# The values of a gated linear attention turned in 32x32 squares and through device memory, in place of TensorE transposes

## The chip, the cores and the metric

The kernel runs on one core of one Trainium2 chip. A core has TensorE (PE in the profile: matmuls; PEld: loads of its weights), VectorE (DVE), ScalarE (ACT), GpSimd (POOL) and SyncE (SP), which here issues nearly all transfers. Engines work side by side, each through its own list of instructions. The metric is the time of one execution in microseconds (us); lower is better.

## The reference, cut to what matters

Two layers of an encoder over 272 rows (256 tokens and 16 meta tokens), width 2048, in fp32. Each layer projects the stream once, runs gated linear attention (4 heads, key width 128, value width 256) beside a neighbourhood attention (16 heads), projects back, and ends with a squared-ReLU MLP of width 8192.

```python
proj = jnp.einsum('bld,dp->blp', h, w_in)
gq, gk, gv, gr, glr, nq, nk, nv = jnp.split(proj, points, axis=-1)
...
scores = jnp.einsum('bhtd,bhsd,bhtsd->bhts', qi, ki, decay)
intra = jnp.einsum('bhts,bhse->bhte', scores, vi)
```

The change concerns `gv`, the values: 4 heads of 256 columns. The projection makes them with the columns on the 128 partitions and the 272 rows along a partition; the product with the scores wants them the other way round, rows on the partitions.

## The kernel before

**Weights.** All weights come in tiles of 128 x 1024 floats (512 KB), always in the same way. SP loads a tile into `raw` (`made`, L195). ACT rounds it to the fast matmul type as `wh` (L218), DVE makes the remainder `wl` (L219). `raw`, `wh` and `wl` have three buffers each, so SP can load a tile only when DVE is done with the tile three before it, and ACT can convert a tile only when PE is done with the tile three before it. `weights` keeps two tiles ready ahead of the one in use.

**Projection.** `by_m` makes 128 columns at a time: two weight tiles, each used by `eight` (L253) for 8 blocks with three matmuls per block (`wh` on the high part of the stream, `wh` on its low part, `wl` on the high part), 24 matmuls in all. In the second layer, where only 256 rows are wanted, the q columns take two matmuls per block, `wh` and `wl` in turn, 16 in all. The order inside a tile is "hlhlww" or "hwhw...": the first kind needs `wl` at the fifth matmul, the second at the second.

**The stage around the change.** For each layer, `by_k` makes the keys and the first four value chunks (c0 to c3), then `by_m` makes the value chunks c4 to c7 and after them the four q chunks. In what follows the weight tiles of these `by_m` runs are numbered: T0 and T1 make c4, T2 and T3 c5, T4 and T5 c6, T6 and T7 c7; T8 and T9 make the first q chunk, T10 and T11 the second. Between the tiles, `pump` lets other work take a step: the generator `gates` (the low-rank decays: a projection of 32 matmuls at L469, small matmuls at L487, and on ACT and DVE a chain of abs, exp, ln, min and exp per head, L488 to L493), and for each head `v_rows`.

**The values.** `ev_v` copies a chunk from PSUM to `ft` (L504). When both chunks of a head are there, `v_rows` transposes them on PE with an identity (6 matmuls a head, L517), and `split` and `stack` read the result from PSUM: ACT writes the high part `V` (L339), DVE the low part, which lies in the tiles y12 to y15 (L340); the 16 meta rows go to `VS`, twice high by ACT (L345) and once low by DVE (L346). `gla_head` uses them later as matmul weights (L716 to L720).

**Order.** Each engine's instructions stand in one list that the building framework makes from the code and from what each instruction depends on; waits are on counters that other engines and transfers raise. An engine works through its list from the front, so an instruction that waits holds up all that stand behind it. SP's list in this stage is hardly more than the loads of L195.

Of the kernel before, what the change touches and what calls it, by code (L numbers as in the profile page):

```python
# [38 lines left out]
PAD = 40  # L39
PITCH = 288  # L40
WIDE = 1280
HIGHS = {"once": (0, P, 2 * P), "two": (0, P, 2 * P), "all": (0, P, 2 * P), "all2": (0, P, 2 * P), "own2": (0, P + 48, 2 * P + 64)}
# [16 lines left out]
class Trunk:  # L59
# [127 lines left out]
    def made(self, ap, ends, kind):  # L187
        if ap is None:
            return None
        nc = self.nc  # L190
        raw = self.wp.tile([P, WB], F32, name="raw", tag="raw")
        wh, wl = (self.wp.tile([P, WIDE], F32R, name=nm, tag=nm) for nm in ("wh", "wl"))
        wh, wl = self.blocks(wh, *HIGHS[kind]), self.blocks(wl, *LOWS[kind])
        for c in map(slice, (0,) + ends, ends):
            nc.sync.dma_start(raw[:, c], ap[:, c])  # L195
# [157 lines left out]
    def layer(self, l):  # L353
# [4 lines left out]
        with ExitStack() as actx:  # L358
# [7 lines left out]
            self.decay = [t(f"dec{h}", [P, 2, L]) for h in range(GH)]  # L366
            self.V = a.tile([P, 2 * GH, 2, P], F32R, name="V", tag="V")
            self.vlow = [self.pair(self.yp, "y", 12 + h).both.rearrange("p a c -> p (a c)") for h in range(GH)]
            self.VS = a.tile([80, GH * GDV], F32R, name="VS", tag="VS")
            nc.gpsimd.memset(self.VS.bitcast(F32), 0.0)  # L370
            self.y, self.gate, self.done, self.vt = [None] * DC, {}, set(), []
            if l:
# [6 lines left out]
            with ExitStack() as ectx:  # L379
# [9 lines left out]
                for m, ps in enumerate(first):  # L389
                    self.ev_v(m, ps[0])  # L390
                self.credit, self.alone = 0, True
                self.by_m(self.x, [L] * 4, lambda m, ps: self.ev_v(4 + m, ps), pump=(1, 1, True))
                self.by_m(self.x, [n] * 4, self.ev_q, pump=(1, 1, True))
# [108 lines left out]
    def ev_v(self, c, ps):  # L502
        vt = self.ep.tile([P, L], F32, name="ft", tag="ft", bufs=4)
        self.nc.scalar.copy(vt, ps)  # L504
        self.vt.append(vt)
        if c % 2:
            (self.fg if c > 3 else self.bg).append(self.v_rows(c // 2, self.vt[-2:]))

    def v_rows(self, h, vt):

        nc = self.nc
        yield True
        pt = self.spare(2)
        for i in range(3):
            n = P if i < 2 else NM
            for e in range(2):
                nc.tensor.transpose(pt[e][:n, i * P:i * P + P], vt[e][:, i * P:i * P + n], self.ident)  # L517
# [61 lines left out]
    def gla_head(self, h):  # L579
# [132 lines left out]
        for e in range(2):  # L712
            o = self.bank()[:, :n]
            for i in range(2):
                v, vl = self.V[:, 2 * h + e, i, :], self.vlow[h][:, e * T + i * P:e * T + i * P + P]
                nc.tensor.matmul(o, lhsT=v, rhs=high[:, i, :], start=not i, stop=False)  # L716
# [469 lines left out]
def layout(inputs):  # L1186
# [95 lines left out]
```

## Time and profile before

| | |
|---|---|
| three executions | 2322.43, 2322.55, 2327.5 us; median 2322.55 us |
| profiled execution | 2326.07 us, its span 2324.3 us, mean granted TensorE clock 0.998 |
| PE busy | 2308.5 us (99%), weight loads 2192.0 us (94%) |
| DVE, ACT, POOL busy | 1536.8 us (66%), 1223.4 us (53%), 125.9 us (5%) |
| transfers | 431.65 MB, mean 186 GB/s |
| value and q stage, first layer | about 53 to 93 us |
| value and q stage, second layer | about 1242 to 1285 us |

A group's row in the profile names line, engine, operation, what is written and read, the shape and the count; behind the bar stand the busy time in us, the mean duration of one in ns, and the idle time of the engine just before them with what ended it. A row of the timeline has the start and the length in us, then the same names. In the rows of the windows the engines' busy time comes with the count of instructions in brackets, then the granted clock (PEclk).

### The profile page before, as it was taken

The numbers are of one execution on the slowest core, as the hardware profiler recorded it, in microseconds if no ns is written. First come the engines' busy times: TensorE is split into PE (matmuls) and PEld (weight loads), VectorE is DVE, ScalarE is ACT, GpSimd is POOL, SyncE is SP. The second block draws the span as 40 slices with busy tenths as digits, with TensorE's granted clock in tenths as the row PEclk, the third lists the DMA queues.
The fourth block names the chain that finished last, engine by engine and source line by source line (L and its number), as shares of the span: only waits on it lengthen the run. The fifth ranks groups of instructions, "written<-read, shape, count | busy, mean of one in ns | idle before, by whom it ended". The sixth has DMA issues, their size and how long they took to land.

```text
span 2324.3 us, 45263 instructions
## 1 busy us (share of the span) xinstructions
PE 2308.5 (99%) x18412; PEld 2192.0 (94%) x18412; DVE 1536.8 (66%) x2456; ACT 1223.4 (53%) x2096; POOL 125.9 (5%) x200
## 2 busy tenths in 40 slices
PE   9999999999999999999999999999999999999998
PEld 9999999999999999999999899989988888888888
DVE  5588887775544455557576788878866545666655
ACT  5666664564433344444456767655654334555443
POOL 0022100110000000000020011100100000000000
PEclk9999999999999999999999999999999999999999
DMA  8555665566665556666655656666666666666664
GB/s 258 155 164 184 196 187 169 170 185 179 179 180 181 182 178 178 180 181 179 179 179 164 181 173 204 210 185 182 198 192 193 192 195 191 192 197 218 195 196 148
DMA packets 129824, 431.65 MB, mean 186 GB/s; under 512 B 14792, under 2 KB 23496, under 8 KB 129616
## 3 DMA queue, kind: packets, MB, share of 16 engines
q1 hardware_dynamic: 117808, 415.65, 59.4%
q10 hardware_dynamic: 11808, 13.11, 1.7%
q8 instruction: 144, 2.36, 0.4%
q14 instruction: 64, 0.52, 0.1%
HBM read 420.32 MB, written 8.39 MB: 184 GB/s over the span
## 4 chain that ended last, share of the span: by engine, by line
PE 91%; DVE 5%; ACT 1%; issue 1%; DMA 1%; ACTq 0%; DVEq 0%; POOL 0%
PE mm L253 52%; PE mm L265 30%; PE mm L304 4%; PE mm L314 2%; DVE wl L219 2%; PE bg L304 1%; DMA raw<-in_win 1%; ACT wh L218 0%; PE bg L851 0%; DVE S L614 0%; PE bg L628 0%; PE bg L469 0%; DVE acc L423 0%; DVE ns L787 0%; ACT ns L756 0%
## 5 line engine op out<-in xcount | busy, mean ns | idle before, releaser
L219 DVE TENSOR_TENSOR wl<-raw,wh 128x1024 fp32r<-128x1024 f32 (+1 forms) x770 | 937.4, 1224 | 626.4 <-ACT wh L218 519.8
L218 ACT CAST wh<-raw 128x1024 fp32r<-128x1024 f32 (+1 forms) x770 | 805.3, 1047 | 757.7 <-PE mm L253 353.3
L253 PE MATMUL mm<-x,wh 128*128 128x272 f32 (+3 forms) x4544 | 806.1, 294 | 0.0
L253 PEld LDWEIGHTS mm<-x,wh 128*128 128x128 f32 x4544 | 647.1, 188 | 15.6 <-issue 0.5
L253 PE MATMUL mm<-x,wl 128*128 128x272 f32 (+3 forms) x2432 | 520.7, 284 | 4.0 <-DVE wl L219 3.9
L253 PEld LDWEIGHTS mm<-x,wl 128*128 128x128 f32 x2432 | 390.7, 188 | 5.5 <-DVE wl L219 5.5
L253 PE MATMUL mm<-y,wh 128*128 128x272 f32 (+1 forms) x1440 | 235.0, 285 | 0.0
L253 PEld LDWEIGHTS mm<-y,wh 128*128 128x128 f32 x1440 | 199.7, 188 | 0.1
L265 PE MATMUL mm<-x,wh 128*128 128x512 f32 x832 | 193.8, 390 | 0.0
L265 PEld LDWEIGHTS mm<-x,wh 128*128 128x128 f32 x832 | 154.3, 188 | 31.0
L253 PE MATMUL mm<-u,wh 128*128 128x272 f32 (+1 forms) x1056 | 172.1, 285 | 0.0
L265 PE MATMUL mm<-y,wh 128*128 128x512 f32 x688 | 162.3, 389 | 0.0
L265 PEld LDWEIGHTS mm<-y,wh 128*128 128x128 f32 x688 | 128.6, 188 | 26.9 <-issue 0.4
L253 PE MATMUL mm<-y,wl 128*128 128x272 f32 (+1 forms) x720 | 146.4, 284 | 0.0
L253 PEld LDWEIGHTS mm<-u,wh 128*128 128x128 f32 x1056 | 146.3, 188 | 0.0
L265 PE MATMUL mm<-u,wh 128*128 128x512 f32 x496 | 118.3, 391 | 0.0
L253 PEld LDWEIGHTS mm<-y,wl 128*128 128x128 f32 x720 | 112.5, 188 | 0.0
L265 PEld LDWEIGHTS mm<-u,wh 128*128 128x128 f32 x496 | 90.9, 188 | 17.7
L253 PE MATMUL mm<-u,wl 128*128 128x272 f32 (+1 forms) x528 | 107.3, 284 | 0.0
L265 PEld LDWEIGHTS mm<-x,wl 128*128 128x128 f32 x832 | 98.4, 188 | 2.0
L265 PE MATMUL mm<-x,wl 128*128 128x256 f32 x832 | 98.8, 276 | 0.0
L265 PEld LDWEIGHTS mm<-y,wl 128*128 128x128 f32 x688 | 84.3, 188 | 2.9
(273 smaller groups left out, 2274.9 us busy)
## 6 DMA issues: line engine op xcount, KB each, us to landing
raw<-in_wff SPq DMA_DIRECT2D x512, 512.0 KB, 3.6
raw<-in_win SPq DMA_DIRECT2D x190, 512.0 KB, 4.1
raw<-in_wout SPq DMA_DIRECT2D x64, 512.0 KB, 4.1
hop<-nt ACTq DMA_DIRECT2D x16, 384.0 KB, 2.4
np<-hop ACTq DMA_DIRECT2D x64, 96.0 KB, 4.8
nb<-in_nab SPq DMA_DIRECT2D x16, 352.0 KB, 4.9
xraw<-in_xT SPq DMA_DIRECT2D x7, 272.0 KB, 5.0
out<-out SPq DMA_DIRECT2D x5, 256.0 KB, 3.0
```

Of the source, the lines that this page charges most:

```text
L218: self.nc.scalar.copy(h, r)
L219: self.wl = self.nc.vector.tensor_tensor(lo, r, h.bitcast(F32), ALU.subtract).ins
L253: mm(o, lhsT=self.block(w, j), rhs=rhs, start=first and not i, stop=last and i == len(TURNS[once]) - 1)
L265: self.nc.tensor.matmul(o, lhsT=self.block(both[j // 8][low], j % 8), rhs=rhs, start=first and not i + j, stop=bool(last and i and j == 15 ...
L304: self.nc.tensor.matmul(ps[g + m][:, :n], lhsT=self.block(parts[p][0], 4 * j + m if first else 2 * m + j), rhs=acts[k + j][parts[p][1]][:, ...
L314: self.nc.tensor.matmul(o, lhsT=self.block(both[low], i), rhs=rhs, start=not low and k + i % 2 == 0, stop=k == DC - 2 and i % 2 == 1 and n ...
```

## The change

PE no longer transposes the values. `ev_v` copies a chunk into a buffer of 288 columns (GpSimd clears the last 16), and DVE turns it in 32x32 squares into `vt`. A new generator, `v_flow`, walks once through the heads with three kinds of steps: `w` writes a head's `vt` to device memory (one transfer on ACT's queue, 288 KB); `r` reads it back as rows, one transfer for each of the eight 32-row blocks (32 KB each, 256 bytes at a time) and one for the meta rows, all nine on SP's queue behind the last weight load asked for so far; `s` makes the high part on ACT, the low part in place on DVE, and `VS`. The steps are w0 w1 r0 w2 r1 s0 r2 w3 s1 r3 s2 s3. The meta rows `vm` have two buffers. The value columns of `w_in` are put in another order on the host, so that the squares come out right, and `gla_head` takes its slices from the new layout with the same matmuls.

```diff
@@ made
-            nc.sync.dma_start(raw[:, c], ap[:, c])
+            self.asked = nc.sync.dma_start(raw[:, c], ap[:, c]).ins
@@ layer
-            self.V = a.tile([P, 2 * GH, 2, P], F32R, name="V", tag="V")
+            self.V = a.tile([P, GH, 2, GDV], F32R, name="V", tag="V")
...
+                self.bg.append(self.v_flow())
                 self.by_m(self.x, [L] * 4, lambda m, ps: self.ev_v(4 + m, ps), pump=(1, 1, True))
@@ ev_v, v_rows
-        vt = self.ep.tile([P, L], F32, name="ft", tag="ft", bufs=4)
-        self.nc.scalar.copy(vt, ps)
-        self.vt.append(vt)
-        if c % 2:
-            (self.fg if c > 3 else self.bg).append(self.v_rows(c // 2, self.vt[-2:]))
-
-    def v_rows(self, h, vt):
-        nc = self.nc
-        yield True
-        pt = self.spare(2)
-        for i in range(3):
-            n = P if i < 2 else NM
-            for e in range(2):
-                nc.tensor.transpose(pt[e][:n, i * P:i * P + P], vt[e][:, i * P:i * P + n], self.ident)
-        for e in range(2):
-            self.split(pt[e][:, :T], self.V[:, 2 * h + e].rearrange("p i c -> p (i c)"), self.vlow[h][:, e * T:e * T + T])
-            self.stack(pt[e][:NM, T:T + P], self.VS[:, h * GDV + e * P:h * GDV + e * P + P], NM, (0, 32), 64)
-            yield
+        e = c % 2
+        if not e:
+            self.vt = self.ep.tile([P, VR, 2, 32], F32, name="vt", tag="vt", bufs=2)
+        t = self.ep.tile([P, VR * 32], F32, name="ft", tag="ft", bufs=2)
+        self.nc.scalar.copy(t[:, :L], ps)
+        self.nc.gpsimd.memset(t[:, L:], 0.0)
+        self.nc.vector.transpose(self.vt[:, :, e, :], t)
+        if e:
+            self.vts.append(self.vt)
+
+    def v_flow(self):
+        nc, ep = self.nc, self.ep
+        hops, metas = {}, {}
+
+        def w(h):
+            hops[h] = self.hp.tile([P, VR, 64], F32, name="vhop", tag="vhop")
+            nc.scalar.dma_start(hops[h], self.vts[h].rearrange("p j e c -> p j (e c)"))
+
+        def r(h):
+            raw = self.vlow[h][:, :2 * T].bitcast(F32).rearrange("p (i a c) -> p i a c", i=2, a=4)
+            metas[h] = ep.tile([NM, GDV], F32, name="vm", tag="vm", bufs=2)
+            at = hops[h].rearrange("(a k) j c -> k j a c", a=4)
+            with self.tc.issue_after(self.asked):
+                for j in range(VR - 1):
+                    nc.sync.dma_start(raw[j % 4 * 32:j % 4 * 32 + 32, j // 4], at[:, j])
+                nc.sync.dma_start(metas[h].rearrange("p (a c) -> p a c", a=4), at[:NM, VR - 1])
+
+        def s(h):
+            low, to = self.vlow[h][:, :2 * T], self.VS[:, h * GDV:h * GDV + GDV]
+            high = self.V[:, h].rearrange("p i c -> p (i c)")
+            nc.scalar.copy(high, low.bitcast(F32))
+            nc.vector.tensor_tensor(low, low.bitcast(F32), high.bitcast(F32), ALU.subtract)
+            self.stack(metas[h], to, NM, (0, 32), 64)
+
+        for f, h in ((w, 0), (w, 1), (r, 0), (w, 2), (r, 1), (s, 0), (r, 2), (w, 3), (s, 1), (r, 3), (s, 2), (s, 3)):
+            while len(self.vts) <= h:
+                yield
+            f(h)
+            yield
@@ layout
+    v = v.reshape(v.shape[:2] + (GH, 4, 2, 32)).transpose(0, 1, 2, 4, 3, 5).reshape(v.shape)
```

Where the instructions stand now is shown at three places. The names carry buffer numbers, which differ between the two programs; which tile is meant is said each time.

ACT, first layer, around the copy of chunk c7. Before, T8 is `wh_1093`, T9 `wh_1139`, T10 `wh_1174`, and `ft_1122<-mm_1061` is the copy of c7:

```order
L345 CAST VS_95<-mm_1000 16x128 x2
L218 CAST wh_1093<-raw_1092 128x1024
L493 ACTIVATE dec3_89<-gt_1046 128x544
L218 CAST wh_1139<-raw_1138 128x1024
L218 CAST wh_1174<-raw_1173 128x1024
L504 COPY ft_1122<-mm_1061 128x272
```

After, T8 is `wh_1116` and the copy of c7 is `ft_1145<-mm_1074`; lines of the changed kernel have other numbers (L219 is the conversion, L509 the copy, L522 the step `w`):

```order
L536 CAST V_90<-y14_93 128x512
L346 CAST VS_95<-vm_1105 16x256 x2
L509 COPY ft_1145<-mm_1074 128x272
L522 DMA vhop_1149<-vt_1052 128x576
L219 CAST wh_1116<-raw_1115 128x1024
L219 CAST wh_1153<-raw_1152 128x1024
```

The conversion of T8 stood four places ahead of the copy of c7; now it stands behind that copy and behind the step `w` of the last head. In the second layer it is the same move. Before, T8 is `wh_15735` and the copy of c7 `ft_15764<-mm_15691`:

```order
L218 CAST wh_15735<-raw_15734 128x1024
L490 ACTIVATE gt_15676<-gt_15676,one_661 128x544
L488 ACTIVATE gt_15724<-bg_15722 128x272
L488 ACTIVATE gt_15724<-bg_15723 128x272
L218 CAST wh_15768<-raw_15767 128x1024
L489 ACTIVATE gt_15724<-gt_15724 128x544
L493 ACTIVATE dec2_14750<-gt_15676 128x544
L490 ACTIVATE gt_15724<-gt_15724,one_661 128x544
L504 COPY ft_15764<-mm_15691 128x272
```

After, T8 is `wh_15774` and the copy `ft_15803<-mm_15720`:

```order
L536 CAST V_14768<-y14_14771 128x512
L509 COPY ft_15803<-mm_15720 128x272
L346 CAST VS_14773<-vm_15763 16x256
L495 ACTIVATE dec3_14767<-gt_15753 128x544
L522 DMA vhop_15807<-vt_15698 128x576
L219 CAST wh_15774<-raw_15773 128x1024
```

T8's conversion has moved from eight places ahead of the copy of c7 to four behind it.

ACT, first layer, between the conversions of T5 and T6. Before (T5 is `wh_958`, T6 `wh_1013`) four instructions of the gates stand between them:

```order
L218 CAST wh_958<-raw_957 128x1024
L488 ACTIVATE gt_897<-bg_895 128x272
L488 ACTIVATE gt_897<-bg_896 128x272
L489 ACTIVATE gt_897<-gt_897 128x544
L490 ACTIVATE gt_897<-gt_897,one_661 128x544
L218 CAST wh_1013<-raw_1012 128x1024
```

After (T5 is `wh_971`, T6 `wh_1023`) eighteen stand between them, of which these are the last ten, ahead of T6:

```order
L522 DMA vhop_967<-vt_812 128x576
L491 ACTIVATE gt_957<-gt_957 128x544
L536 CAST V_90<-y13_92 128x512
L492 ACTIVATE gt_957<-gt_957,one_661 128x544
L490 ACTIVATE gt_1002<-bg_1000 128x272
L490 ACTIVATE gt_1002<-bg_1001 128x272
L346 CAST VS_95<-vm_1012 16x256
L491 ACTIVATE gt_1002<-gt_1002 128x544
L495 ACTIVATE dec1_87<-gt_957 128x544
L492 ACTIVATE gt_1002<-gt_1002,one_661 128x544
L219 CAST wh_1023<-raw_1022 128x1024
```

T6's conversion now stands behind the gates of two more heads, the step `w` of the third head and the high part of the second.

SP, first layer. Before, the loads of T5 (`raw_957`) to T11 (`raw_1205`) stand one behind the other:

```order
L195 DMA raw_957<-in_win 128x1024
L195 DMA raw_1012<-in_win 128x1024
L195 DMA raw_1062<-in_win 128x1024
L195 DMA raw_1092<-in_win 128x1024
L195 DMA raw_1138<-in_win 128x1024
L195 DMA raw_1173<-in_win 128x1024
L195 DMA raw_1205<-in_win 128x1024
```

After, from the load of T5 (`raw_970`) to that of T11 (`raw_1229`), with T8 as `raw_1115`:

```order
L196 DMA raw_970<-in_win 128x1024
L530 DMA y13_92<-vhop_866 32x4x64 x8
L531 DMA vm_1012<-vhop_866 16x4x64
L196 DMA raw_1022<-in_win 128x1024
L196 DMA raw_1075<-in_win 128x1024
L530 DMA y14_93<-vhop_967 32x4x64 x8
L531 DMA vm_1105<-vhop_967 16x4x64
L196 DMA raw_1115<-in_win 128x1024
L196 DMA raw_1152<-in_win 128x1024
L196 DMA raw_1187<-in_win 128x1024
L530 DMA y15_94<-vhop_1149 32x4x64 x8
L531 DMA vm_1218<-vhop_1149 16x4x64
```

The nine reads of the third head now stand ahead of the load of T8, and those of the fourth head ahead of the load of T11; the reads of a head wait there for its write.

More of the change, by code (lines that the diff above doesn't have):

```diff
@@ L40 @@
 PITCH = 288
+VR = 9
 WIDE = 1280
@@ L370, in layer @@
             nc.gpsimd.memset(self.VS.bitcast(F32), 0.0)
-            self.y, self.gate, self.done, self.vt = [None] * DC, {}, set(), []
+            self.y, self.gate, self.done, self.vts = [None] * DC, {}, set(), []
             if l:
@@ L714, in gla_head @@
             for i in range(2):
-                v, vl = self.V[:, 2 * h + e, i, :], self.vlow[h][:, e * T + i * P:e * T + i * P + P]
+                c = slice(e * P, e * P + P)
+                v, vl = self.V[:, h, i, c], self.vlow[h][:, i * T:i * T + T][:, c]
                 nc.tensor.matmul(o, lhsT=v, rhs=high[:, i, :], start=not i, stop=False)
```

## The prediction

> **What bounds the kernel now.** I read the page first (busy time, chain), then the stage around the change (windows, timeline), then single groups.
>
> ```profile
> PE 2308.5 (99%) x18412; PEld 2192.0 (94%) x18412; DVE 1536.8 (66%) x2456; ACT 1223.4 (53%) x2096; POOL 125.9 (5%) x200
> PE 91%; DVE 5%; ACT 1%; issue 1%; DMA 1%; ACTq 0%; DVEq 0%; POOL 0%
> ...
> 53.00:93.20 40.20, 40.20 (x331) 39.80 (x329) 23.48 (x37) 29.04 (x59) 0.32 (x1) 1.00 0.48 144
> 1242.40:1284.90 42.50, 42.50 (x323) 40.69 (x321) 25.53 (x41) 30.04 (x61) 0.31 (x1) 1.00 0.52 157
> ```
>
> PE never rests: in both value stages (the last two rows, T0 to T10 with all transposes) it is busy all the time. The second engine is ACT, 29.04 of 40.20 us or 72%, far above its 53% of the whole. So a matmul less is a gain in full, and a conversion of weights that comes late is a loss in full. How late it may come is read from the timeline, layer 1 and then layer 2:
>
> ```profile
> 81.45 1.05 ACT L218 CAST wh<-raw 128x1024 fp32r<-128x1024 f32 x1
> 82.54 1.23 DVE L219 TENSOR_TENSOR wl<-raw,wh 128x1024 fp32r<-128x1024 f32 x1 [0.36 <-ACT wh L218]
> 82.97 1.98 ACT L218 CAST wh<-raw 128x1024 fp32r<-128x1024 f32 x2
> 83.08 0.82 PE L517 MATMUL mm<-ident,ft 128*128 128x128 f32 x6
> 83.66 0.75 PE L253 MATMUL mm<-x,wh 128*128 128x272 f32 x4
> 84.85 0.38 ACT L504 COPY ft<-mm 128x272 f32<-128x272 f32 x1
> ...
> 92.61 0.82 PE L517 MATMUL mm<-ident,ft 128*128 128x128 f32 x6
> ...
> 1269.54 1.03 ACT L218 CAST wh<-raw 128x1024 fp32r<-128x1024 f32 x1
> 1272.49 0.40 PE L253 MATMUL mm<-x,wh 128*128 128x512 f32 x1
> 1272.73 0.28 PE L253 MATMUL mm<-x,wl 128*128 128x256 f32 x1
> 1274.37 0.37 ACT L504 COPY ft<-mm 128x272 f32<-128x272 f32 x1
> 1275.29 0.82 PE L517 MATMUL mm<-ident,ft 128*128 128x128 f32 x6
> ```
>
> T8's conversion is the first row: begun 2.21 us before T8's first matmul at 83.66, its `wl` done at 83.77, where the fifth matmul wants it about 0.5 later. In layer 2 it begins 2.95 us ahead (1269.54 against 1272.49). The copy of c7 comes after both, at 84.85 and 1274.37, though c7 was complete at about 83.1 and 1272.5. From 83.66 to 92.61 PE does three tiles: 2.98 us each, 0.124 a matmul. Six transposes cost the 0.58 us from 83.08 to 83.66. Layer 2's T8, to 1275.29, takes 2.80.
>
> **The change, part by part.**
>
> *Removed from PE:* 48 transposes, 8 groups of 0.58: -4.6 us, all on the path.
>
> *Exchanged on ACT and DVE.* ACT loses small reads of PSUM and gains eight wide copies, 16 `VS` copies and 8 issues; DVE gains 16 square turns and 8 wide low parts. The rows for the prices:
>
> ```profile
> L218 ACT CAST wh<-raw 128x1024 fp32r<-128x1024 f32 (+1 forms) x770 | 805.3, 1047 | 757.7 <-PE mm L253 353.3 <-PE mm L265 178.7 <-DMA raw<-in_wff 70.3
> L219 DVE TENSOR_TENSOR wl<-raw,wh 128x1024 fp32r<-128x1024 f32 (+1 forms) x770 | 937.4, 1224 | 626.4 <-ACT wh L218 519.8 <-issue 95.0 <-PE bg L858 2.5
> L345 ACT CAST am<-Am 16x272 fp32r<-16x272 f32 (+1 forms) x16 | 6.6, 410 | 0.3
> L488 ACT ACTIVATE gt<-bg 128x272 f32<-128x272 f32 x16 | 5.5, 391 | 0.0
> L489 ACT ACTIVATE gt<-gt 128x544 f32<-128x544 f32 x8 | 5.3, 662 | 0.1
> L490 ACT ACTIVATE gt<-gt,one 128x544 f32<-128x544 f32 x8 | 6.1, 757 | 0.2
> L493 ACT ACTIVATE dec<-gt 128x544 f32<-128x544 f32 x8 | 5.3, 659 | 0.0
> L658 ACT COPY S<-qk 128x544 f32<-128x544 f32 x8 | 5.2, 649 | 0.0
> L799 DVE STREAM_TRANSPOSE nt<-npr x16: 395/414/433, 200.7 to 1521.0; 128x256 f32<-128x256 f32 x16
> L820 ACTq DMA_DIRECT2D hop<-nt x16: 344/344/349, 201.2 to 1521.5; - x16
> DMA to landing us min/median/max: 2.3/2.4/4.3
> ```
>
> The sums on these engines hardly move and cost nothing while PE's time covers them; places in the lists do cost. GpSimd's 16 clears lie beside a GpSimd busy 5%. The later head products keep their matmuls. The write of a head is like `hop<-nt` (2.4 us to landing, the last row).
>
> *T8, first layer.* Its conversion stands behind the copy of c7 and step `w` of head 4, and the copy needs T7's last matmul. So from T7's end: copy 0.38, turn on DVE 0.45 (288 columns against 0.414 for 256), issue 0.34, `wh` 1.05, `wl` 1.22, and four hand-overs of 0.04 (82.50 to 82.54): 3.6 us, less 0.5 of matmuls that need only `wh`: PE waits **3.1 us**. Nothing else can cover it, for no other matmul is free in PE's list.
>
> *T8, second layer.* Copy 0.38, `VS` 0.41, decay 0.66, issue 0.34, `wh` 1.05, `wl` 1.22, less about 0.2 where ACT's neighbours overlap, less the 0.24 to the second matmul (1272.49 to 1272.73): 3.6; ACT gets to the copy about 0.4 late by its list. **4.0 us.** For both the low end is 3.0 and 3.6. The high end is the meta read of head 3: SP can issue it only when DVE has used up the first `vm` (two buffers), about 3.9 us before T7's end; ACT's `VS` in front waits for it.
>
> ```profile
> L826 ACTq DMA_DIRECT2D np<-hop x64: 309/310/1377, 203.5 to 1527.4; - x64
> DMA to landing us min/median/max: 2.1/4.8/7.5
> raw<-in_win SPq DMA_DIRECT2D x190, 512.0 KB, 4.1
> 32.34 0.33 SPq L195 DMA_DIRECT2D raw<-in_win  x1
> 32.71 0.43 SPq L89 DMA_DIRECT2D vec<-in_vec  x1
> 73.16 0.26 PE bg L487 x2
> ```
>
> A read of this kind landed after 2.1 to 7.5 us; at 7.5, T8 is 3.6 us later in each layer. I take the near end: `np` is 768 bytes a piece and beside ACT's traffic, these are 256.
>
> *T6.* From T2's end, ACT does T5's `wh`, six L488, three L489, three L490, two decays, a copy, a high part (like L658), a `VS` and an issue: 1.05 + 2.35 + 1.99 + 2.27 + 1.32 + 0.38 + 0.65 + 0.41 + 0.34 = 10.8, less an overlap of 0.1 (two `wh` take 1.98) at some half of 19: 9.7. With `wh`, `wl` and hand-over 12.0. PE needs 3 x 2.98 + 4 x 0.25 (L487) + 0.5 = 10.4. **1.5 us** (0.7 to 2.6). In layer 2, from T3's end, the same count gives 7.6 against 7.2: **0.4** (0 to 1.5).
>
> *SP.* 72 reads of some 0.37 us (32.34 to 32.71), nine at a time. Reads of heads 1 and 2 delay loads that have microseconds to spare while PE does L469. Those of head 4 wait for its write: in layer 1 it is issued 1.2 after T7's end, lands at 3.6, the reads are out at 7.0, T11's load lands 4.1 later, converted at 13.4. PE wants it at 3.1 + 8.95 + 0.5 = 12.6: **0.8 us**; layer 2 likewise 14.4 against 12.6: **1.8** (0 to 4 each).
>
> *The clock.* A rest of PE can cost a second time:
>
> ```profile
> 326.16 0.53 PE L253 MATMUL mm<-x,wl 128*128 128x272 f32 x2 [1.68 <-DVE wl L219]
> ...
> 353.73 0.87 PE L851 MATMUL bg<-np,v 64*64 64x128 f32 x12 [1.40 <-DMA np<-hop]
> 359.82 1.11 PE L304 MATMUL mm<-y,wh 128*128 128x272 f32 x4
> 361.18 1.11 PE L304 MATMUL mm<-y,wh 128*128 128x272 f32 x4
> ...
> 352.10:355.50 3.40, 2.00 (x25) 1.76 (x25) 0.35 (x1) 0.18 (x1) 0.00 (x0) 1.00 1.03 276
> 355.50:362.30 6.80, 6.80 (x39) 6.51 (x39) 2.17 (x4) 1.77 (x4) 0.00 (x0) 0.50 0.34 104
> ```
>
> After a rest of 1.40 us the granted clock stood at 0.50 for 6.8 us: six matmuls from 359.82 to 361.18, 0.227 each against 0.124, a loss of 3.1 us; a rest of 1.68 at 324.5 cost no clock. T8's rests are twice that, so I expect a fall in each layer, 3.0 us. T11 then comes late enough for its load, and those two waits vanish.
>
> The Trainium skill speaks here too ("TensorE: Matmul & The Clock Gate", "HAM oscillation — how this bites in real kernels"): it asks for no gaps above about 3.4 us, and by that rule T8's rests, broken by the first matmuls, would cost no clock. The fall after 1.40 us speaks against it, the rest of 1.68 for it. By the rule the sum would be +7.0, the first rival below.
>
> *Sum:* -4.6 + 1.5 + 3.1 + 0.4 + 4.0 + 2 x 3.0 = **+10.4 us**. The profiled execution took 2326.07 (its span 2324.3), 3.5 above the median of 2322.55; there it would be 2336.5, at the median **2333.0**.
>
> **Rivals.**
> 1. *The clock stays up.* Then T11's waits count: -4.6 + 1.5 + 3.1 + 0.8 + 0.4 + 4.0 + 1.8 = +7.0, 2329.6. For it: the rest of 1.68. With one fall out of two, +8.7 on the mean of the two sums.
> 2. *Only the two forced waits.* ACT's list runs closer together, reads land in 2.1, no clock falls: -4.6 + 7.1 = +2.5, 2325.1.
> 3. *The reads land late.* At up to 7.5 us the meta read holds ACT, and all conversions behind it: +10.4 and up to 2 x 3.6, some 2341.
> 4. *Not slower:* PE does not wait at T8. Place: ACT, at the copy of c7. If a weight tile more were converted when T7 ends, only the gain would be left: 2318.0. It decides once all waits together are under 4.6 us. Against it: three buffers, and T8's conversion is listed behind c7.
>
> Saved time alone never reaches 0.3% (7 us, about what a measurement of this kernel can tell from no change); faster by more would need the old fall at 355.5 to vanish as well (3.1).
>
> **How the numbers follow.** Forecast, two falls, 42%; one fall 14%; rival 1 16%; rival 2 8%; rival 3 17%; rival 4 3%. Slower by over 0.3% is above 2329.5: nearly all of the forecast, three quarters of one fall, half of rival 1, all of rival 3: 0.74. Faster: 0.02. The rest, 0.24, lies within. From 2325 (rival 2) to 2341 (rival 3) some 9 in 10 of the cases have a place, 8 with their own spread.
>
> **What would show it.** Right: no L517; PE's idle time before T8's first matmul 2 to 3 us in each layer, released by the conversion, and about 1 more before the first `wl` matmul; ACT's copy of c7 right ahead of the issue and the conversion; windows of granted clock 0.50, some 6.8 us long, near 90 and 1280. Wrong: T8 starting within 0.5 us of T7's end; or PE waiting for loads (T8's or T11's by the transfer) longer than for ACT's list.

## The result, and the profile after

The changed kernel takes 2341.62 us (median of six executions, 2337.0 to 2343.17); the kernel before, run beside it, 2323.94 (2322.43 to 2327.5). The ratio on record is 1.0066, with a 95% interval of 1.0055 to 1.0078: some 15 us slower (the two medians lie 17.7 us apart, at the upper end of the interval; what follows goes by the ratio). Put on the 2322.55 us of the prediction, that is 2337.9 us: 4.9 above the forecast of 2333.0, inside the range of 2325 to 2341, and slower by more than 0.3%.

The profiled execution took 2342.54 us, its span 2340.7, 16.4 more than the span before. The page after: the engines, the chain, and the two new transfers (KB each, median us from issue to landing).

```profile
PE 2310.4 (99%) x18364; PEld 2190.9 (94%) x18364; DVE 1540.7 (66%) x2456; ACT 1221.5 (52%) x2072; POOL 129.5 (6%) x216
PE 85%; DVE 6%; DMA 3%; ACT 3%; issue 2%; SPq 1%; POOL 0%; ACTq 0%; DVEq 0%; POOLq 0%
...
vhop<-vt ACTq DMA_DIRECT2D x8, 288.0 KB, 4.8
y<-vhop SPq DMA_DIRECT2D x64, 32.0 KB, 1.9
```

PE has 48 instructions fewer. In the chain its share falls from 91% to 85%; transfers and ACT rise from 1% to 3% each, and SP's queue comes in with 1%. The windows of the two value stages show PE at rest where it never rested before: 5.20 us of 43 in the first layer, 7.28 of 56 in the second, each with the granted clock below 1 (0.92, 0.94).

```profile
53.00:96.00 43.00, 37.80 (x276) 36.58 (x276) 21.96 (x34) 25.53 (x47) 0.77 (x6) 0.92 0.50 147
1244.00:1300.00 56.00, 48.72 (x349) 44.93 (x348) 29.33 (x45) 34.81 (x62) 1.46 (x10) 0.94 0.52 158
```

PE's own timeline names the places (in brackets the rest just before and what ended it). The first three are T6 (two rows) and T8 of the first layer; then, in the second, the small gate products at L489, which stand four matmuls into T4, T8 (two rows), and T11.

```profile
77.86 0.77 PE L254 MATMUL mm<-x,wh 128*128 128x272 f32 x4 [2.10 <-ACT wh L219]
79.12 0.82 PE L254 MATMUL mm<-x,wl 128*128 128x272 f32 x2 [0.49 <-DVE wl L220]
88.71 1.20 PE L254 MATMUL mm<-x,wh 128*128 128x272 f32 x4 [2.55 <-ACT wh L219]
...
1267.35 0.49 PE L489 MATMUL bg<-lr,up 98*128 98x272 f32 x2 [2.42 <-DVE lr L347]
...
1283.40 0.75 PE L254 MATMUL mm<-x,wh 128*128 128x512 f32 x1 [2.75 <-ACT wh L219]
1284.66 0.58 PE L254 MATMUL mm<-x,wl 128*128 128x256 f32 x1 [0.51 <-DVE wl L220]
1296.52 0.50 PE L254 MATMUL mm<-x,wh 128*128 128x512 f32 x1 [0.63 <-ACT wh L219]
```

The stretches of granted clock 0.50 in the windows of the same trace (the clock stands behind POOL's column):

```profile
78.58:81.99 3.41, 2.92 (x13) 2.87 (x13) 3.15 (x6) 3.27 (x7) 0.00 (x0) 0.50 0.07 15
88.81:92.22 3.41, 3.35 (x14) 3.03 (x15) 3.35 (x5) 1.74 (x2) 0.00 (x0) 0.50 0.18 43
361.88:365.29 3.41, 3.41 (x24) 3.37 (x20) 0.51 (x1) 1.04 (x1) 0.00 (x0) 0.50 0.25 95
1283.48:1290.31 6.83, 6.32 (x19) 5.04 (x20) 4.59 (x5) 2.29 (x3) 0.00 (x0) 0.50 0.32 69
```

The clock fell behind T6 and T8 of the first layer for 3.41 us each, and behind T8 of the second for 6.83; the old fall, at 355.5 before, is half as long.

**Where the time went.** Both kernels make the same projection matmuls in the same order, so the start of the n-th of them in one trace less its start in the other is the delay gathered up to there. In the changed kernel it grows by 7.3 us through the first layer's value stage (from -0.2 at 53 us of the trace before to 7.1 at 98), falls by 1.0 up to the second layer, where the old clock fall is half as long, grows by 9.4 through the second stage (6.1 to 15.5), and by 0.9 behind it. Read from tile to tile, the steps are +4.3 in T6 and +4.0 in T8 of the first layer, and in the second +2.3 in T4 (with L489), +5.7 in T8 and +1.6 in T11; where a group of six transposes is gone and nothing waits, it falls by 0.7.

**What came late.** SP's queue in the first layer, and below it the load of T5 in the kernel before:

```profile
52.18 0.33 SPq L196 DMA_DIRECT2D raw<-in_win  x1
58.01 4.56 SPq L530 DMA_DIRECT2D y<-vhop  x8
62.61 0.43 SPq L531 DMA_DIRECT2D vm<-vhop  x1
63.14 0.37 SPq L196 DMA_DIRECT2D raw<-in_win  x1
```

```profile
55.30 0.33 SPq L195 DMA_DIRECT2D raw<-in_win  x1
```

After the load at 52.18 SP stands 5.5 us, until the first head's write, issued at 52.93, has landed, then issues nine reads in 5.0 us; T5's load is issued at 63.14 instead of 55.30. In the second layer it goes the same way (SP stands from 1249.5 to 1254.7, T5's load is issued at 1259.67), and ACT's list shows what follows:

```profile
1260.88 0.62 ACT L536 CAST V<-y 128x512 fp32r<-128x512 f32 x1 [5.18 <-DMA vm<-vhop]
1261.41 0.82 ACT L346 CAST VS<-vm 16x256 fp32r<-16x256 f32 x2
1263.64 1.05 ACT L219 CAST wh<-raw 128x1024 fp32r<-128x1024 f32 x1 [1.42 <-DMA raw<-in_win]
1264.72 0.38 ACT L476 COPY lrt<-bg 32x272 f32<-32x272 f32 x1
1266.33 0.86 ACT L346 CAST lr<-lrt 32x272 fp32r<-32x272 f32 x2 [1.23 <-DVE lrt L477]
```

ACT waits 5.18 us for the first head's reads to land and 1.42 for T5's load; behind both stands the copy `lrt` of the low-rank chain, whose product PE had finished at about 1261.5. From 1266.33 to T8's conversion at 1282.31 ACT is busy for 15.43 of 15.98 us: it carries the lost time with it as a backlog, and T8's conversion is the next place where PE runs out of work. Whether SP's queue is the cause, or ACT's list with the copy of c7 ahead of T8's conversion, as the prediction had it, is what the experiments were to tell.

### The profile page after: what moved, and what is told of

Its sections match the earlier page's. It is cut to its first block, busy times and chain, and to the rows that moved or that the text cites. A ratio compares the mean times of both kernels' runs of the same rounds, so it can differ in the third digit from the quotient of the medians.

```text
span 2340.7 us, 45323 instructions
## 1 busy us (share of the span) xinstructions
PE 2310.4 (99%) x18364; PEld 2190.9 (94%) x18364; DVE 1540.7 (66%) x2456; ACT 1221.5 (52%) x2072; POOL 129.5 (6%) x216
## 4 chain that ended last, share of the span: by engine, by line
PE 85%; DVE 6%; DMA 3%; ACT 3%; issue 2%; SPq 1%; POOL 0%; ACTq 0%; DVEq 0%; POOLq 0%
PE mm L254 48%; PE mm L266 29%; PE mm L305 3%; DVE wl L220 2%; DMA raw<-in_win 2%; PE mm L315 2%; PE bg L305 1%; ACT wh L219 1%; DMA np<-hop 1%; DVE S L637 1%; SPq L530 1%; DMA vhop<-vt 1%; PE bg L875 0%; DVE acc L425 0%; ACT ns L780 0%
## 5 line engine op out<-in xcount | busy, mean ns | idle before, releaser
L219 ACT CAST wh<-raw 128x1024 fp32r<-128x1024 f32 (+1 forms) x770 | 804.7, 1047 | 756.4 <-PE mm L254 339.0
L266 PEld LDWEIGHTS mm<-u,wh 128*128 128x128 f32 x496 | 90.9, 188 | 17.7
```

What stands on the lines that cost most here:

```text
L219: self.nc.scalar.copy(h, r)
L266: self.nc.tensor.matmul(o, lhsT=self.block(both[j // 8][low], j % 8), rhs=rhs, start=first and not i + j, stop=bool(last and i and j == 15 ...
```

## Experiments

Line numbers shift by a few between the kernels. The delay through a stage is measured as above, on the profiled execution against that of the kernel before; the ratio is over all executions.

| kernel | median us | ratio to before (95%) | stage of layer 1 | stage of layer 2 |
|---|---|---|---|---|
| changed kernel | 2341.62 | 1.0066 (1.0055 to 1.0078) | +7.3 | +9.4 |
| copy of a chunk behind the conversion | 2339.46 | 1.0065 (1.0051 to 1.0079) | +1.8 | +11.0 |
| reads off SP | 2325.74 | 1.0006 (0.9998 to 1.0015) | -2.2 | +3.0 |
| no way through memory | 2317.43 | 0.9972 (0.9962 to 0.9982) | -2.8 | -2.7 |
| the same, reads alone | 2326.49 | 1.0009 (1.0001 to 1.0018) | -0.1 | +2.4 |
| four meta buffers | 2339.57 | 1.0072 (1.0058 to 1.0085) | +6.9 | +9.0 |
| four meta buffers, copy behind | 2339.64 | 1.0068 (1.0054 to 1.0081) | +2.7 | +12.9 |
| late `s`, reads on SP | 2339.40 | 1.0063 (1.0051 to 1.0076) | +5.3 | +7.4 |
| late `s`, reads off SP | 2318.18 | 0.9976 (0.9967 to 0.9986) | -2.8 | -2.6 |
| late `s`, later reads on SP | 2330.64 | 1.0025 (1.0016 to 1.0034) | -0.8 | +3.9 |
| late `s`, two reads a head on SP | 2324.01 | 1.0000 (0.9991 to 1.0008) | -0.6 | +2.6 |
| late `s`, two reads a head on GpSimd | 2319.15 | 0.9976 (0.9966 to 0.9986) | -2.8 | -2.7 |

The two last columns leave something out. Between the first stage and 300 us of the trace another 2.6 us gather with the copy behind, 2.4 with four buffers and the copy behind, 3.1 with the later reads, and 1.1 and 1.2 in the two kernels with nine reads a head off SP; what PE waits for there was not followed up. And of these traces only the changed kernel's still has the old clock fall, at 361.88; without it the other eleven gain 2.6 to 3.8 us between the stages, whatever their edit. The kernel before has executions with a granted clock of 1.0 too (one of 2322.4 us) beside the profiled one (2326.07 us, 0.998). A clock fall in a single trace is therefore in part chance.

### ACT's list or SP's queue

First the prediction's own cause: the copy of c7 is put back behind T8's conversion, and nothing else is changed.

```diff
 def halves(self, src, wh, wl, at):
-    self.nc.scalar.copy(h, r)
+    self.wh = self.nc.scalar.copy(h, r).ins
...
 def ev_v(self, c, ps):
-    self.nc.scalar.copy(t[:, :L], ps)
+    with self.tc.issue_after(self.wh):
+        self.nc.scalar.copy(t[:, :L], ps)
```

> The changed kernel; the copy of a value chunk is kept behind the newest weight conversion on ACT, so that T8's conversion stands ahead of the copy of c7 in both layers; SP's list is as it was. Theory L: the T8 waits (2.55, and 2.75 with 0.51) and the clock falls behind them (1.7 and 3.1 us lost) go: about 2331 us. Theory Q: T8's load landed at 85.20 in the first layer, 1 us ahead of the copy at 86.24, so the conversion can move forward by about 1 us only; the T6 wait, the wait of the low-rank chain and most of T8's stay, the clock still falls: 2337 to 2341 us.

Measured: 2339.46 us, ratio 1.0065; the changed kernel has 1.0066. Theory L, with its 2331, falls: the order in ACT's list, given back at this place, returns nothing in all that ratios with intervals of this width (some 3 us to either side) can show. It isn't without effect: in the first layer of the profiled execution T8's rest shrank to 1.07 and 0.49, no clock fall followed, and T8 adds 1.4 us instead of 4.0. (T6 adds 2.3 instead of 4.3, mostly because no clock fall followed its rests either.) But the second stage became longer (+11.0), and its rest at T8 stayed:

```profile
1261.81 0.49 PE L489 MATMUL bg<-lr,up 98*128 98x272 f32 x2 [2.18 <-DVE lr L347]
...
1277.88 0.50 PE L254 MATMUL mm<-x,wh 128*128 128x512 f32 x1 [2.77 <-ACT wh L219]
```

There ACT reaches T8's conversion late whether the copy of c7 stands ahead of it or behind, since all of its list is late.

Then the reads are taken off SP's queue.

```diff
-            with self.tc.issue_after(self.asked):
-                for j in range(VR - 1):
-                    nc.sync.dma_start(raw[j % 4 * 32:j % 4 * 32 + 32, j // 4], at[:, j])
-                nc.sync.dma_start(metas[h]...)
+            for j in range(VR - 1):
+                nc.gpsimd.dma_start(raw[j % 4 * 32:j % 4 * 32 + 32, j // 4], at[:, j])
+            nc.gpsimd.dma_start(metas[h]...)
...
-        self.nc.gpsimd.memset(t[:, L:], 0.0)
+        self.nc.vector.memset(t[:, L:], 0.0)
```

> The changed kernel with the nine reads of a head on GpSimd's queue instead of SP's, and the clears of the last 16 columns on DVE, since on GpSimd they would stand behind the reads. In ACT's list T8's conversion then stands six places ahead of the copy of c7 again. Theory Q (SP's queue): the reads stand ahead of weight loads on SP and hold them, first by the wait for the write, then by about 0.47 us each; that makes T6's conversion, the low-rank chain of the second layer and T8's conversion late, and ACT's order only follows from it. PE's idle time in the two value stages (5.3 and 7.3 us) and the two extra clock falls vanish: 2319 to 2324 us, PE idle under 1 us in each stage. Theory L (ACT's list, the prediction): the copy of c7 and the step w ahead of T8's conversion cost the two T8 waits and their clock falls (about 10 us), the waits at T6 and in the low-rank chain stay: about 2331 us. Theory R (reads land late wherever they are issued, and ACT's VS copies wait for them): 2338 us or more, with ACT idle behind vm.

Measured: 2325.74 us, ratio 1.0006. Nearly the whole loss is gone, more than theory L allowed (2331), though it stays 1.7 above the upper end of theory Q. ACT's list, first layer, shows that its order changes with the reads: with them off SP's queue T8's conversion (the first row below; the second is T9's) stands, in the order that ran, seven places ahead of the copy of c7 (the last row; four places before the change).

```profile
79.33 1.07 ACT L219 CAST wh<-raw 128x1024 fp32r<-128x1024 f32 x1
...
81.38 1.06 ACT L219 CAST wh<-raw 128x1024 fp32r<-128x1024 f32 x1
...
83.78 0.37 ACT L509 COPY ft<-mm 128x272 f32<-128x272 f32 x1
```

So this edit changes two things at once, the queue and the order that the framework makes on ACT. No kernel here has the changed kernel's order on ACT with the reads off SP.

What is left lies in the second layer (+3.0): PE's rest at the low-rank chain with a clock fall of 3.41 us behind it, and on ACT what caused the rest. The first three rows are ACT's, the last is PE's.

```profile
1253.72 0.62 ACT L536 CAST V<-y 128x512 fp32r<-128x512 f32 x1 [4.85 <-DMA y<-vhop]
1255.26 0.82 ACT L346 CAST VS<-vm 16x256 fp32r<-16x256 f32 x2 [0.93 <-DMA vm<-vhop]
1256.11 0.38 ACT L476 COPY lrt<-bg 32x272 f32<-32x272 f32 x1
```

```profile
1258.00 0.79 PE L489 MATMUL bg<-lr,up 98*128 98x272 f32 x2 [3.35 <-DVE ft L510]
```

The step `s` of the first head stands in ACT's list ahead of `lrt` and waits for the reads to land: theory R, as a second cost behind SP's queue, not in its place.

### The floor, and the reads alone

```diff
 def w(h):
-    hops[h] = ...
-    nc.scalar.dma_start(hops[h], self.vts[h]...)
+    pass
 def r(h):
-    ...
+    pass
 def s(h):
-    nc.scalar.copy(high, low.bitcast(F32))
-    nc.vector.tensor_tensor(low, low.bitcast(F32), high.bitcast(F32), ALU.subtract)
-    self.stack(metas[h], to, NM, (0, 32), 64)
+    flat = self.vts[h].rearrange("p j e c -> p (j e c)")
+    nc.scalar.copy(high, flat[:, :2 * T])
+    nc.vector.tensor_tensor(low, flat[:, :2 * T], high.bitcast(F32), ALU.subtract)
+    self.stack(flat[:NM, 2 * T - GDV + 64:2 * T + 64], to, NM, (0, 32), 64)
```

This kernel leaves out the order of the rows across the 32-row blocks; it gives a floor for the time and no usable values.

> The changed kernel without the way through device memory: no write, no reads; the high and low parts and VS are made straight from the turned tile (four buffers), so the values stay only partly turned. Left out: the order of the rows across the 32-row blocks. PE, ACT (less the eight issues) and DVE do the same work. Theory Q: nothing is left that makes PE wait, and the 48 transposes are saved: the time before less 4.6, about 2319 us (2318 to 2321). Theory L: T8's conversion stands three places ahead of the copy of c7, so the T8 waits go here too, but the waits at T6 and in the low-rank chain, if they come from the wide copies on ACT, stay: 2325 us or more.

Measured: 2317.43 us, 0.9972: what theory Q had, and half a microsecond more. PE does not rest at all in either stage:

```profile
53.00:96.00 43.00, 43.00 (x351) 42.75 (x350) 28.43 (x42) 31.42 (x57) 0.71 (x5) 1.00 0.51 159
1240.00:1300.00 60.00, 60.00 (x462) 55.07 (x461) 42.45 (x65) 42.71 (x79) 3.14 (x8) 1.00 0.56 167
```

So the square turns, the wide copies and the `VS` copies fit beside PE's work; the gain is 2.8 and 2.7 us in the two stages, for 48 transposes that the prediction had at 4.6, and a little more elsewhere (the fall of the clock at 355.5 is not in this trace).

To this kernel the 72 reads are added again, from an input, waiting for nothing and waited for by nobody:

```diff
 def r(h):
-    pass
+    raw = ep.tile([P, 2, 4, 64], F32, name="junk", tag="junk", bufs=2)
+    vm = ep.tile([NM, 4, 64], F32, name="jm", tag="jm", bufs=2)
+    at = self.i["xT"][:32, :4, :64]
+    with self.tc.issue_after(self.asked):
+        for j in range(VR - 1):
+            nc.sync.dma_start(raw[j % 4 * 32:j % 4 * 32 + 32, j // 4], at)
+        nc.sync.dma_start(vm, at[:NM])
```

> The kernel without the way through device memory, to which the 72 reads on SP's queue are added again as reads of the input of the same shape into a tile that nobody uses; they wait for no write, and nothing waits for them. T8's conversion stands just ahead of the copy of c7. Theory Q: the reads alone hold the loads of T6, T8 and T11 by 4.2 us each: 5 to 18 us slower than without them, 2325 to 2337 us, PE idle for several us in each value stage. Theory L: the loads have the time to spare: within 2 us of the kernel without them.

Measured: 2326.49 us, 9.1 above the kernel without them. Theory L (within 2) falls again. But 9.1 is little more than a third of the 24.2 between the floor and the changed kernel (22 by the ratios): nine issues a head, without any waiting, don't make the whole loss; what the reads wait for, who waits for them, and the order on ACT are left for the larger part.

### The meta buffers

The prediction's high end was that SP can issue a meta read only once DVE has used up an older `vm`. Four buffers take that wait away; the second kernel has the copy behind the conversion as well.

```diff
-            metas[h] = ep.tile([NM, GDV], F32, name="vm", tag="vm", bufs=2)
+            metas[h] = ep.tile([NM, GDV], F32, name="vm", tag="vm", bufs=4)
```

> The changed kernel with four buffers for the meta rows vm instead of two. There SP issued the meta read of the third head only at 1276.65 in the second layer, after a hold of 2.65 us (behind eight reads that ended at 1274.0), and at 80.54 in the first, 3.1 us behind the eight reads; the load of T8 stands behind it. Theory Q: this moves T8's load forward by 2.7 to 3.1 us, but in ACT's list T8's conversion still stands behind the copy of c7 and the step w, so T8's wait stays; the loads of T9 and later gain: no more than 2 us, 2339 to 2342. Rival M (the prediction's high end: the meta read is what makes T8 late): T8's waits shrink by 2 us or more in each layer, with the clock falls: 2335 us or less.

> Both edits: four buffers for the meta rows, and the copy of a value chunk kept behind the newest conversion on ACT. Theory Q: T8 is held by two things at once, the place of its conversion and the late load, and taking both away gives more than the sum of the single gains (2.1 us for the copy alone): T8's conversion starts before T7's end in the first layer (wait under 0.5 instead of 1.07 and 0.49) and up to 2.5 us earlier in the second; the waits at T6 and in the low-rank chain stay: 2332 to 2337 us. If the two gains only add: 2337 to 2340 us.

Measured: 2339.57 and 2339.64 us, ratios 1.0072 and 1.0068. Neither differs from the changed kernel's 1.0066. The rival M falls, and with it the mechanism of the prediction's third rival. The wait itself is there: in the changed kernel's trace SP waits 2.7 us ahead of the third head's meta read in the first layer and 2.6 in the second, with the load of T8 behind it; but nothing in the time hangs on it while the rest is late. The second expectation of theory Q fails as well (2332 to 2337): in the first layer T8 starts nearly on time (its only rest is 0.24 us), as expected, but not in the second, where PE rests 2.78 and 0.76 us at T8 behind 2.52 at the low-rank chain. What holds T8 there is neither the copy of c7 nor its own load (its conversion, at 1279.43, waits for nothing). By ACT's timeline it is the backlog that starts when ACT waits 5.04 us for the first head's reads and 1.67 for T5's load.

### The landing of the reads on ACT

The steps `s` go to the end of the walk, behind the newest conversion; `vm` and `vhop` get four buffers. Once with the reads off SP, once with the reads on SP.

```diff
-        for f, h in ((w, 0), (w, 1), (r, 0), (w, 2), (r, 1), (s, 0), (r, 2), (w, 3), (s, 1), (r, 3), (s, 2), (s, 3)):
+        for f, h in ((w, 0), (w, 1), (r, 0), (w, 2), (r, 1), (r, 2), (w, 3), (r, 3), (s, 0), (s, 1), (s, 2), (s, 3)):
...
 def s(h):
+    with self.tc.issue_after(self.wh):
         nc.scalar.copy(high, low.bitcast(F32))
         ...
```

> Reads on GpSimd's queue and clears on DVE as in the kernel with the reads off SP, and the steps s (high part, low part, VS) at the end of the walk, behind the newest weight conversion on ACT and DVE, with four buffers for the meta rows and in device memory. There ACT stood 4.85 and 0.93 us behind the landing of the first head's reads in the second layer, with the low-rank chain's copy behind it, and PE waited 3.35 us for that chain. Theory W (waiting for a landing in ACT's list is the second cost beside SP's queue): that wait and its clock fall go, nothing is left: 2317 to 2320 us, as the kernel without the way through memory (2317.4), and faster than before. Rival G (72 reads on GpSimd's queue cost by themselves, by the traffic or by GpSimd's work beside DVE): 2323 us or more.

> The changed kernel with the steps s at the end of the walk, behind the newest weight conversion, and four buffers for the meta rows and in device memory; the reads stay on SP's queue. Nothing on ACT or DVE waits for a landing early. Theory Q: the reads still hold the loads, and SP still waits for each write: T6's wait, T8's wait and the clock falls stay; only the wait of the low-rank chain (2.4 us) goes: 2333 to 2339 us. Theory W alone (ACT's waits for the landings are the greater part): the difference to the kernel without the way through memory shrinks to what the reads alone cost there (9.1 us): 2327 us or less.

Measured: 2318.18 us (0.9976, interval 0.9967 to 0.9986) off SP; 2339.40 (1.0063) on SP. The first is faster than the kernel before by a quarter of a per cent, and level with the floor; PE does not rest in either stage, and rival G falls:

```profile
53.00:96.00 43.00, 43.00 (x351) 42.75 (x351) 27.33 (x43) 29.28 (x52) 19.90 (x37) 1.00 0.74 212
1240.00:1300.00 60.00, 60.00 (x465) 55.22 (x464) 41.90 (x67) 44.23 (x80) 22.36 (x42) 1.00 0.72 210
```

On SP the late `s` saves nothing that the ratios show, about what theory Q had (its range ended at 2339). ACT no longer waits for a landing, and waits for T5's load instead (ACT's row below, second layer; then SP's):

```profile
1259.23 1.05 ACT L219 CAST wh<-raw 128x1024 fp32r<-128x1024 f32 x1 [8.12 <-DMA raw<-in_win]
```

```profile
1242.51 2.32 SPq L196 DMA_DIRECT2D raw<-in_win  x2
1249.86 4.81 SPq L530 DMA_DIRECT2D y<-vhop  x8
1254.77 0.38 SPq L531 DMA_DIRECT2D vm<-vhop  x1
1255.24 0.37 SPq L196 DMA_DIRECT2D raw<-in_win  x1
```

So the second cost hides behind the first: while SP holds the loads, waiting for a landing on ACT is free; once the reads are off SP, it costs 7 us (1.0006 against 0.9976). Theory W alone falls. Theory Q misses one point: it had the wait of the low-rank chain go, and it stayed (2.59 us), since T5's load is what it waits for.

### What holds SP: the landing or the nine issues

SP stands for two things in the rows above: until the write has landed (1244.83 to 1249.86), and for nine issues (to 1255.15). One kernel reads two tiles later in the walk, so that the write has nearly landed (SP still stands 1.5 us for it in the first layer and 1.3 in the second):

```diff
-  (w, 0), (w, 1), (r, 0), (w, 2), (r, 1), (r, 2), (w, 3), (r, 3), (s, 0), ...
+  (w, 0), (w, 1), (z, 0), (z, 0), (r, 0), (r, 1), (w, 2), (z, 0), (z, 0), (r, 2), (w, 3), (z, 0), (z, 0), (r, 3), (s, 0), ...
+        def z(h):
+            pass
```

> The kernel with the late steps s and the reads on SP (2339.4 us), with the reads of each head two tiles later in the walk (four buffers hold what waits). SP's first reads then stand behind T5's load instead of ahead of it, and the write that they wait for was issued some 9 us before. Theory H (SP's standing still for the landing of a write is what costs, 12.9 us between the late s on SP and the kernel with the same reads that wait for nothing): SP stands for no write any more, the wait of the low-rank chain in the second layer goes, and the time is that of the kernel with reads that wait for nothing: 2325 to 2330 us. Theory N (nine issues of 0.47 us at a stretch are the cost, wherever they stand): the stall only moves to another tile: 2334 us or more.

The other leaves the reads where they were and lays the array out as rows, so that two reads do for a head:

```diff
-            hops[h] = self.hp.tile([P, VR, 64], F32, name="vhop", tag="vhop", bufs=4)
-            nc.scalar.dma_start(hops[h], self.vts[h].rearrange("p j e c -> p j (e c)"))
+            hops[h] = self.hp.tile([VR, 32, 4, 64], F32, name="vhop", tag="vhop", bufs=4)
+            for a in range(4):
+                nc.scalar.dma_start(hops[h][:, :, a].rearrange("j k c -> k j c"), self.vts[h][32 * a:32 * a + 32]...)
...
-                for j in range(VR - 1):
-                    nc.sync.dma_start(raw[j % 4 * 32:j % 4 * 32 + 32, j // 4], at[:, j])
+                nc.sync.dma_start(raw..., at[:2 * P].rearrange("(i p) f -> p i f", i=2))
```

> The kernel with the late steps s, the reads on SP in their old place, but the array in device memory is laid out as rows: a head is written by four transfers on ACT's queue (one for each 32 partitions) and read by two on SP's (all 256 rows, and the meta rows) instead of nine. SP issues 16 reads instead of 72. Theory N: SP is held for 0.9 us a head instead of 4.2, and little is left: 2325 us or less. Theory H: SP still stands for the landing of each write (5 us behind its issue), T5's load of the second layer with it: 2328 to 2336 us. ACT's 24 further issues of 0.34 us add up to 8 us in its list, beside PE's work if ACT has the room.

Measured: 2330.64 us (1.0025) with the later reads, 2324.01 (1.0000) with two reads, against 2339.40 (1.0063) with neither. Neither theory has both: taking the landing away gives back 8.8 us, where H expected 9 to 14 and N at most 5; taking seven of nine issues away gives back 15.4, where N expected 14 or more and H 3 to 11. Both kernels differ in more than that: the first gathers 3.1 us behind the first stage, the second writes a head in four transfers, and both have another order on ACT. SP's queue with two reads, first layer:

```profile
52.93 0.33 SPq L196 DMA_DIRECT2D raw<-in_win  x1
58.98 0.38 SPq L530 DMA_DIRECT2D y<-vhop  x1
59.42 0.46 SPq L531 DMA_DIRECT2D vm<-vhop  x1
59.97 0.37 SPq L196 DMA_DIRECT2D raw<-in_win  x1
```

SP still stands six microseconds for the landing, and T5's load is still 4.7 us later than in the kernel before (59.97 against 55.30). Yet that costs hardly anything: T5's conversion, at 69.97, does not wait for the load, and PE rests only 0.25 and 0.49 us in this stage. With nine reads and the same late `s`, the load goes out at 63.38, 8.1 us late, and ACT waits 3.00 us for it:

```profile
67.38 1.05 ACT L219 CAST wh<-raw 128x1024 fp32r<-128x1024 f32 x1 [3.00 <-DMA raw<-in_win]
```

There PE rests 1.84 and 0.49 us at T6. So landing and issues add up on SP, and only what goes beyond the load's slack reaches ACT and then PE; for this load the slack lies between 4.7 and 8.1 us. That fits the two gains, 8.8 and 15.4, which together are more than the 21.2 us between this kernel with nine reads and the late `s` off SP. The slack of the other loads was not measured.

The last kernel puts the four writes and two reads of a head on GpSimd's queue (`nc.gpsimd.dma_start` in both places, clears on DVE):

> Writes (four a head) and reads (two a head) all on GpSimd's queue, clears on DVE, late steps s: neither SP nor ACT issues or waits for anything of the way through memory. All theories expect no wait of PE in the value stages: 2316 to 2320 us; the question is whether it is faster than the nine reads on GpSimd's queue with the write on ACT's (2318.2), by up to 2 us for the eight issues that ACT is rid of, or not, since PE waits for neither.

Measured: 2319.15 us, 0.9976 (0.9966 to 0.9986), the same as the late `s` with nine reads off SP. PE rests in neither stage, so fewer transfers and a freer ACT buy nothing more.

## Why the prediction came out as it did

- **Direction and size.** Slower by more than 0.3% was given 0.74, and happened. The sum of +10.4 us stands against +16.4 between the two profiled executions and, by the ratio, about +15 over all runs. By stages it had +5.3 and +5.1; measured are +7.3 and +9.4. That it came so near is partly luck: in the first layer T6 cost 2.8 more than its term and T8 2.1 less, and in the second layer T4 (2.3) and T11 (1.6) cost time that the sum did not have.
- **The saving.** -4.6 was right within a microsecond: without the way through memory the two stages gain 5.5.
- **T8, first layer** (3.1, and 3.0 for the clock). The rest was 2.55 us, then a fall of 3.41 us, a delay of 4.0 in all. Place, releaser and the row of copy, issue and conversion ahead of it are as predicted, and with the copy moved behind the conversion T8's delay fell to 1.4: here the prediction's mechanism was at work. ACT's list there (the copy waits for PE, its own idle time in brackets):

```profile
86.24 0.39 ACT L509 COPY ft<-mm 128x272 f32<-128x272 f32 x1 [1.54 <-PE mm L254]
...
87.24 0.33 ACTq L522 DMA_DIRECT2D vhop<-vt  x1
87.61 2.94 ACT L219 CAST wh<-raw 128x1024 fp32r<-128x1024 f32 x3 [0.98 <-DVE vt L511]
```

- **T8, second layer** (4.0, and 3.0). Rests of 2.75 and 0.51, a fall of 6.83 us, 5.7 in all: near the forecast, for another reason. The prediction took the order of the list as the cause; with the order given back it stayed (copy behind the conversion: 2.77).
- **T6, first layer** (1.5). This term was mis-sized: 2.10 and 0.49, and a clock fall that was not in the sum, 4.3 in all. The count of ACT's work from T5's conversion to T6's (9.7) was good: 67.33 to 76.78 is 9.45. But T5's conversion began 1.08 us late, behind its load; 1.5 and 1.08 make 2.6, which is what PE rested (in the second layer, where the term was 0.4, PE rested 0.21 us at T6):

```profile
67.33 1.05 ACT L219 CAST wh<-raw 128x1024 fp32r<-128x1024 f32 x1 [1.08 <-DMA raw<-in_win]
...
76.78 1.03 ACT L219 CAST wh<-raw 128x1024 fp32r<-128x1024 f32 x1
```

- **The step that failed** is the sentence on SP: "Reads of heads 1 and 2 delay loads that have microseconds to spare while PE does L469." They have, but not enough. The write's landing was taken as 2.4 us, from `hop<-nt`; it is 4.8. A read was taken as 0.37 us; with the pauses between them nine take 4.8 to 5.0. And SP's standing still for the landing ahead of the first head's reads was not counted at all. T5's load came 7.8 us later in the first layer; in the second, `lrt` stood behind T5's conversion, PE rested 2.42 us at L489, a place that the prediction did not name, and ACT began its backlog. The order of ACT's list, which the prediction read as the cause, changed with the reads: off SP, T8's conversion went back ahead of the copy by itself. How much of the loss goes straight through the late loads, and how much through that order, is not shown.
- **T11** (waits that vanish behind the clock falls). In the first layer, yes (0.14 us); in the second it cost 1.6.
- **The clock.** Falls at 88.81 and 1283.48 came where they were expected, the first half as long. One more came behind T6, and the old one at 355.5 halved, which was not foreseen. "The clock stays up" (rival 1) did not happen. The rule of the Trainium skill that the prediction weighed ("TensorE: Matmul & The Clock Gate", "HAM oscillation — how this bites in real kernels"), no gaps above about 3.4 us, does not hold here: all four falls followed rests of 1.94 to 2.75 us.
- **Rivals.** The third gave a time near the measured one (2341), but its mechanism, the meta read that holds ACT, is not it: with four buffers nothing changed. Rivals 2 and 4 did not happen.

## What to carry to other kernels

A queue that feeds the bound engine is the wrong place for a transfer that has to wait: everything behind it stands as long as it does, and the order that the framework then made on another engine looked like the whole cause. Put such transfers on a queue whose standing still hurts nobody; if they must stay, make them few; and place what consumes them late in every engine's list. Here the two steps together turned 15 us of loss into 6 of gain. The first alone gave back 14, and the second alone nothing that could be measured, since its cost was hidden behind the first. Count a load's slack in microseconds, and add up the landing that a queue waits for and every issue ahead of the load, before calling a transfer hidden.

## What was not expected of the hardware

- Reads on GpSimd's queue cost PE nothing here, once nothing waited for them early. The Trainium skill ("DMA: Bandwidth & Descriptors", "Issuing engines are not separate DMA queues") says that starting transfers from several engines saves only the time to initiate them, usually small. Here the move took the ratio from 1.0066 to 1.0006. What it saved on SP was, for the first head, nine issues (4.8 to 5.0 us) and the standing still ahead of them (5.3 to 5.5 us): more than the issues, and neither is small beside a load's 4.3 us to its landing.
- The clock falls of one trace start on a grid: 78.58, 88.81, 361.88 and 1283.48 are 3, 80 and 270 times 3.413 us apart. The Trainium skill ("TensorE: Matmul & The Clock Gate", "What's actually happening") has a free-running window of 3413 ns, which agrees. Its idle window as the condition does not: rests of 2.10, 2.55, 1.94 and 2.75 us, each inside one such window, were enough for a fall at its end, while the 2.42 us before 1267.35, which the grid cuts into 1.48 and 0.94, brought none. Shorter, broken rests did bring one in other traces (0.70 and 0.77 us at T8 with two reads), so the condition itself stays open.
- A write of 288 KB to device memory landed after 4.8 us (`vhop`, median of eight), one of 384 KB before the change after 2.4 (`hop`). Why the smaller one takes longer is open.
